# Two-block transformer on one core: norm sums of the last mixer taken at the end of the first expert stage, and the spatial unit's dense product placed behind the keys

## The chip, the cores and the metric

The kernel runs on one core of a Trainium2 chip. The metric is the device time of one execution in microseconds (us); less is better. The core has five engines that run side by side, each in the order of its own instruction list: TensorE (PE, with its weight loads shown apart as PEld), VectorE (DVE), ScalarE (ACT), GpSimd (POOL) and SyncE (SP). SP does no arithmetic here: it issues the weight transfers. An engine waits at an instruction until the semaphores that it needs have come, and everything behind it in its list waits too.

## The reference

Two blocks follow each other on the same 256 tokens of 1024 channels. Block A (two layers and a final rmsnorm with a gain) isn't touched. Block B has two layers; each runs a mixer and then a mixture of experts (16 experts, each takes 32 tokens). Layer 0 does it for the tokens `x` and for 256 context tokens `xc`; layer 1 takes from the context only keys and values.

```python
def rms_norm(x):
    return x * lax.rsqrt(jnp.mean(x * x, axis=-1, keepdims=True) + EPS)

def modulate_2(x, shift, scale):
    return rms_norm(x) * (1 + scale) + shift

x = rmsnorm(x_of_block_A, final_norm)          # end of block A
for l in range(2):
    hx = modulate_2(x, sh1, sc1);  hc = modulate_2(xc, csh1, csc1)
    px = hx @ w_in[l]              # columns u 256, v 256, f 256, q 256, kv 128, kr 64
    pc = hc @ w_in[l][:, col0:]    # last layer: kv and kr alone
    ya = gelu(u) * spatial(rms_norm(gelu(v)))  # spatial unit
    yb = fft2(f).real
    q  = rope(rms_norm(rms_norm(px_q) @ w_uq))
    k, v = rms_norm(px_kv) @ w_ukv, ...        # tokens and context
    x  = x + g1 * (concat(ya, yb, attention(q, k, v)) @ w_out[l])
    x  = x + g2 * expert_choice_moe(modulate_2(x, sh2, sc2), ...)
    # layer 0 does the last lines for xc too
```

At the start of block B's layer 0 two norms follow each other: the final rmsnorm of block A, with a gain, and the rms_norm of the mixer.

## The kernel before

Activations are held transposed: `xT` and `xcT` are 128 partitions (channels within a group) by 8 groups of channels by 256 tokens, in fp32. A dense product is done with split operands: `split` (L314, L315) makes from 1024 columns of a weight a rounded part `wsh` on ACT and the rest `wsl` on DVE, and `mm3` makes three matmuls of each pair of tiles (L322 high by high, then L323 and L324 with one low part each). There are two buffers each for `wsh` and `wsl`, so a third split waits until PE has used up the first.

Block B is driven by a plan, one string for each layer (`PLAN`, L53 and L54), whose words are traced in their order. `x0` and `x1` make the modulated norms of tokens and context; `v0` the dense product with the weight `wvf` (columns v and f); `u0` that with `wu` (the spatial unit's u); `tj` the one with `wqk` (the low-rank columns q, kv, kr) for tokens and context; `nj` the norms of these low-rank rows and their transposes (L1337 to L1360); `fj` the Fourier product; `k1` and `k0` keys and values of context and tokens (L1371 to L1401); `q0` the queries (L1418 to L1440); `a..` one head of attention (from L1504); `sj`, `w0`, `p0`, `r0` the spatial product, the output product, the router's norm and the routing. `F` fills in products of modulation vectors (L473, evicted at L477 or L479). A scheduler then sets the order in which each engine runs the traced instructions, so a word that is moved in one layer's plan, and a sum that is traced elsewhere, can move instructions of the other stages too.

A norm's sums of squares are made by `sums` (L608 on): eight Squares on ACT (L615), eight fp32 matmuls with a block of ones (L617), which the trace records as two each, a transpose on DVE (L619), one matmul that gathers (L621). `inv_sqrt` (L627) and `rsqrt` (L594 to L606, nine small DVE operations) follow, then `spread` (a COPY, L637, and a transpose, L639, on DVE). `modulated` multiplies on DVE (L664), adds the shift on ACT (L665, `hh`) and takes the low part on DVE (L666, `hl`).

In layer 0 the two norms are done as one chain on the tokens: sums of x, first inverse root `y1`, sums of x times the gain, second inverse root from `y1` and these. The first inverse root also rescales `xT` in place (L1592).

Expert weights come in pieces of 2 MB through a ring of buffers (`slot`, L281); SP issues a transfer (L294) when the buffer's last reader is done. At the end of layer 0's expert stage each half of the last results is added to `xT` and then `xcT` (L1891).

## Time and profile before

| | us |
|---|---|
| median of 3 runs | 1552.39 (1551.93 to 1553.54) |
| profiled execution | 1550.65 |
| its span, first to last instruction | 1548.9 |
| PE busy | 1425.8 (92%) |
| DVE busy | 894.8 (58%) |
| ACT busy | 578.5 (37%) |
| 16 DMA engines moved | 434.09 MB, mean 280 GB/s |
| mean granted TensorE clock | 0.975 of full |

In the span, block A runs to about 700 us. Block B's layer 0 begins its mixer there and its experts at about 940; layer 1 begins at about 1190, its experts at 1347. Times in the rows are us from the span's start. In a row of a timeline the first number is the start, the second the time until the last of its instructions ended, then engine, line, operation, output and inputs (buffer numbers left out), shapes and how many instructions the row holds; in brackets, how long the engine had been idle before and what it waited for. One matmul's time includes its passage through the array, so the distance of two starts is what it costs in a row of matmuls.

### The profile page before, as it was taken

The page shows a single profiled execution, that of the slowest core. Times are in us where ns is not written, and L with a number is a line of the kernel's source. Part 1 is how long each engine was busy: PE and PEld are TensorE (multiplying, and loading weights), DVE is VectorE, ACT ScalarE, POOL GpSimd, SP SyncE. Part 2 cuts the span into 40 slices and gives each one's busy share as a digit, 9 for nine tenths or more (in the row PEclk, how much of TensorE's full clock was granted, in tenths as well). Part 3 has the DMA queues.
Part 4 walks back from the last instruction along what each step waited for, and adds up shares of the span by engine and source line. Part 5 has one row for each costly group of instructions (what it writes and reads, how often), then busy time and mean ns, then how long its engine had stood idle before and what let it go on. Part 6 is the DMA issues. An engine that isn't in the chain of part 4 may idle for free.

```text
span 1548.9 us, 25284 instructions
## 1 busy us (share of the span) xinstructions
PE 1425.8 (92%) x10360; PEld 990.0 (64%) x10362; DVE 894.8 (58%) x2051; ACT 578.5 (37%) x1180; POOL 5.0 (0%) x15
## 2 busy tenths in 40 slices
PE   5999999999999999999999999999998889897665
PEld 2965899997967999996754784443433656632111
DVE  5668788896776998966665542322224765422011
ACT  3455444443555444544654441211102564310000
POOL 0000000000000000000000000000000000000000
PEclk9999999999999999999999999999999999999788
DMA  9647678597424866554286976899993225699998
GB/s 396 261 178 297 261 275 323 216 394 302 179 110 162 313 259 233 210 210 171 113 315 252 404 305 251 329 414 388 415 368 162 110 109 198 276 428 428 427 427 341
DMA packets 33666, 434.09 MB, mean 280 GB/s; under 512 B 3728, under 2 KB 4368, under 8 KB 6032
## 3 DMA queue, kind: packets, MB, share of 16 engines
q1 hardware_dynamic: 32400, 429.92, 69.8%
q10 hardware_dynamic: 1152, 2.57, 0.5%
q8 instruction: 81, 1.33, 0.3%
q14 instruction: 33, 0.27, 0.0%
HBM read 431.43 MB, written 1.05 MB: 279 GB/s over the span
## 4 chain that ended last, share of the span: by engine, by line
PE 75%; DMA 10%; DVE 9%; ACT 2%; issue 1%; POOLq 0%; DVEq 0%; ACTq 0%; SPq 0%
PE g L322 13%; PE g L324 13%; PE g L323 13%; PE g L1838 7%; PE y L1875 5%; DMA raw<-in_md_dram 4%; PE t L473 3%; DMA raw<-in_mgu_dram 3%; DMA h<-in_mgu_dram 3%; DVE wsl L315 2%; PE m L1838 2%; PE t L1797 2%; PE y L1506 1%; PE g L1523 1%; PE y L1504 1%
## 5 line engine op out<-in xcount | busy, mean ns | idle before, releaser
L314 ACT ACTIVATE wsh<-raw 128x1024 fp32r<-128x1024 f32 (+4 forms) x236 | 242.8, 1033 | 316.4 <-PE g L323 233.9
L315 DVE TENSOR_TENSOR wsl<-raw,wsh 128x1024 fp32r<-128x1024 f32 (+4 forms) x236 | 279.5, 1188 | 88.9 <-ACT wsh L314 88.2
L322 PE MATMUL g<-h,wsh 128*128 128x256 f32 x1072 | 303.8, 286 | 3.7 <-ACT h L657 2.4
L324 PE MATMUL g<-h,wsl 128*128 128x256 f32 x1072 | 304.1, 285 | 2.0 <-DVE wsl L315 2.0
L323 PE MATMUL g<-h,wsh 128*128 128x256 f32 x1072 | 303.9, 285 | 0.2
L322 PEld LDWEIGHTS g<-h,wsh 128*128 128x128 f32 x1072 | 205.1, 192 | 9.5 <-ACT h L665 3.2
L324 PEld LDWEIGHTS g<-h,wsl 128*128 128x128 f32 x1072 | 205.6, 192 | 3.9 <-DVE wsl L315 2.8
L323 PEld LDWEIGHTS g<-h,wsh 128*128 128x128 f32 x1072 | 205.9, 192 | 1.4 <-DVE h L666 0.6
L1838 PE MATMUL g<-raw,xs 128*32 128x512 f32 x1232 | 165.2, 626 | 20.4 <-DMA raw<-in_mgu_dram 19.8
L1875 PE MATMUL y<-raw,a 128*32 128x512 f32 x736 | 99.9, 631 | 9.3 <-DMA raw<-in_md_dram 8.4
L1838 PEld LDWEIGHTS g<-raw,xs 128*32 128x32 f32 x1232 | 38.8, 112 | 106.6 <-issue 70.4
L324 PE MATMUL g<-gh,wsl 128*128 128x256 f32 x352 | 99.8, 284 | 1.5 <-DVE wsl L315 1.5
L322 PE MATMUL g<-gh,wsh 128*128 128x256 f32 x352 | 100.1, 284 | 0.0
L323 PE MATMUL g<-gl,wsh 128*128 128x256 f32 x352 | 99.8, 283 | 0.0
L438 DVE CUSTOM_DVE_ANT_0 raw<-raw,crowc,cols 128x1024 f32<-128x1024 f32 x64 | 80.7, 1280 | 1.2 <-DMA raw<-in_mod1t_dram 1.1
L473 PE MATMUL t<-raw,zc 128*32 128x512 f32 x512 | 71.4, 611 | 6.9 <-DMA raw<-in_mod_dram 6.9
L1802 ACT ACTIVATE xs<-t,modada,ra 128x128 f32<-128x128 f32 x32 | 14.6, 457 | 151.3 <-PE t L1797 107.7
L324 PEld LDWEIGHTS g<-gh,wsl 128*128 128x128 f32 x352 | 67.5, 192 | 1.9 <-DVE wsl L315 1.9
L322 PEld LDWEIGHTS g<-gh,wsh 128*128 128x128 f32 x352 | 67.5, 192 | 1.6 <-issue 1.2
L323 PEld LDWEIGHTS g<-gl,wsh 128*128 128x128 f32 x352 | 67.5, 192 | 0.8 <-issue 0.8
L1875 PEld LDWEIGHTS y<-raw,a 128*32 128x32 f32 x736 | 23.7, 113 | 64.3 <-issue 42.6
L1800 DVE TENSOR_SCALAR xs<-t,ra,modada 128x128 f32<-128x128 f32 x32 | 13.1, 410 | 87.6 <-PE t L1797 50.4
(480 smaller groups left out, 2327.3 us busy)
## 6 DMA issues: line engine op xcount, KB each, us to landing
raw<-in_mgu_dram SPq DMA_DIRECT2D x61, 2048.0 KB, 13.7
raw<-in_md_dram SPq DMA_DIRECT2D x28, 2048.0 KB, 12.0
raw<-in_ffgu_dram SPq DMA_DIRECT2D x22, 2048.0 KB, 8.9
raw<-in_ada_dram SPq DMA_DIRECT2D x19, 2048.0 KB, 7.8
raw<-in_mod_dram SPq DMA_DIRECT2D x12, 2048.0 KB, 9.5
raw<-in_mod1t_dram SPq DMA_DIRECT2D x11, 2048.0 KB, 9.7
raw<-in_ffd_dram SPq DMA_DIRECT2D x16, 1408.0 KB, 7.1
raw<-in_win_dram SPq DMA_DIRECT2D x6, 2048.0 KB, 12.6
```

Of the source, the lines that this page charges most:

```text
L314: self.nc.scalar.activation(hi, src, AF.Copy)
L315: self.nc.vector.tensor_tensor(lo, src, hi.bitcast(F32), op=ALU.subtract)
L322: mm(out, ah, bh, start=first, stop=False)
L323: mm(out, ah, bl, start=False, stop=False)
L324: mm(out, al, bh, start=False, stop=last)
L438: nc.vector.tensor_tensor_reduce(junk, w[:, q, :], zr[:, i, :], 0.5, self.cols[:, o + 4 * s + q:o + 4 * s + q + 1], ALU.mult, ALU.add, m[: ...
L473: nc.tensor.matmul(acc[32 * j:32 * j + 32, :], zw[:, k, :], w[:, k, :], start=(k < 4), stop=(k >= 4))
L1504: nc.tensor.matmul(sc, self.qT[:, hd, ts], self.kT[:, hd, :nk], start=True, stop=False)
L1506: nc.tensor.matmul(sc, self.qrT[s2, hd // 2, ts], self.krT[s2, hd // 2, :nk], start=False, stop=True)
L1797: nc.tensor.matmul(ps, s["ht"][:, t, k * 128:(k + 1) * 128], oh[:, t, :], start=(t == 0), stop=(t == 1))
L1838: nc.tensor.matmul(banks[si][u][32 * e:32 * e + 32, :], xs[:, k, e * 32:e * 32 + 32], raw[:, u * 2048 + e * 512:u * 2048 + e * 512 + 512], ...
L1875: nc.tensor.matmul(ys[si][32 * e:32 * e + 32, :], hts[si][:, f * 128 + 32 * e:f * 128 + 32 * e + 32], raw[:, (fj * 4 + e) * 512:(fj * 4 + ...
```

## The change

Three things are done, all in block B.

1. Sums for layer 1's mixer are traced at the end of layer 0's expert stage, behind the last addition to `xT` and behind that to `xcT` (`sums2`). They use another form: each squared tile is the stationary operand, 128 by 128, and a two-column selector the moving one, so the sums of 256 tokens come out as 128 by 2, with the mean and epsilon already in; `spread2` takes the inverse root on these two columns (one DVE operation fewer) and spreads it by two matmuls with a broadcast operand into PSUM, from where `modulated` reads it. The DVE transposes and the COPY of `sums` and `spread` go in these two places. A word `E` at the plan's start makes the first two splits of `wvf`.
2. In layer 0 the two roots no longer depend on each other. With a prepared gain `gfin`, the root of g squared plus epsilon, the combined norm needs one sum alone; the first norm's sum, which rescales `xT`, is traced behind it.
3. `u0` stands behind `k0` in layer 1's plan, in front of `q0`, where it stood in front of `tj`. The transfer of `wu` moves with it: SP issues it behind `wqk` and `sm` (the weights of the attention's projections) instead of in front of them, and half of `wo` lands in the buffer `h` instead of a ring buffer.

```diff
-EX = 0
...
 PLAN = ['F1 +Q x1 x0 tj +U F2 nj uj v0 ...
-        '+U x0 x1 v0 u0 +H +Q F2 tj nj F1 +A1 -A fj k1 k0 F1 q0 a03 F1 sj F5 a02 a00 F1 a01 -B3 p0 w0 -W2 r0']
+        'E +U x0 x1 v0 +H +Q F2 tj nj F1 +A1 -A fj k1 k0 u0 F1 q0 a03 F1 sj F5 a02 a00 F1 a01 -B3 p0 w0 -W2 r0']
...
+        self.epsc = self.t(c, [128, 2], F32, "epsc")
+        nc.vector.memset(self.epsc, EPS)
+        self.sel2 = self.t(c, [128, 2, 2], F32, "sel2")
+        nc.vector.memset(self.sel2, 0.0)
+        for t in range(2):
+            nc.vector.memset(self.sel2[:, t, t:t + 1], 1.0)
...
+        nc.vector.tensor_tensor(self.gfin, g, g, op=ALU.mult)
+        nc.vector.tensor_scalar(self.gfin, self.gfin, EPS, None, op0=ALU.add)
...
+        self.rsqrt(y, c, t, c)
+        nc.vector.tensor_tensor(self.gfin, self.gfin, y, op=ALU.mult)
...
+    def sums2(self, x):
+
+        nc = self.nc
+        ps = self.ps(self.stag)[:, :2]
+        nk = x.shape[1]
+        nc.tensor.matmul(ps, self.ident, self.epsc, start=True, stop=False)
+        for k in range(nk):
+            sq = self.w([128, 256], "a256", NA2)
+            nc.scalar.activation(sq, x[:, k, :], AF.Square, scale=1.0 / 32)
+            for t in range(2):
+                nc.tensor.matmul(ps, sq[:, t * 128:t * 128 + 128], self.sel2[:, t, :], start=False, stop=(k == nk - 1 and t == 1))
+        return ps
+
+    def spread2(self, cp):
+
+        y = self.w([128, 2], "rsy2", 2)
+        self.rsqrt(y, cp, self.w([128, 2], "rst2", 2), self.w([128, 2], "rsc2", 2))
+        r = self.ps("y")[:, :256]
+        for t in range(2):
+            self.nc.tensor.matmul(r[:, t * 128:t * 128 + 128], y[:, t:t + 1].to_broadcast([128, 128]), self.ident, start=True, stop=True)
+        return r
...
-            w = self.split(raw[:, k0 * 512:(k0 + 2) * 512], 1024)
+            w = self.pre.pop(0) if self.pre else self.split(raw[:, k0 * 512:(k0 + 2) * 512], 1024)
...
-            self.h[1] = self.hc if l == 0 else self.modulated(xc, self.scale_cols(mn, 1, None, 1), mn, 0, 1, later=VX > 0)
+            r = self.spread2(self.early.pop(1)) if l else None
+            self.h[1] = self.hc if l == 0 else self.modulated(xc, self.scale_cols(mn, 1, None, 1), mn, 0, 1, r=r, later=VX > 0)
...
-            r = (self.rx if EX == 2 else self.spread(self.inv_sqrt(self.rx, 1024))) if EX else None
+            r = self.spread2(self.early.pop(0))
...
-            y1 = self.inv_sqrt(self.sums(x), 1024)
-            s2 = self.sums(x, gain)
-            v = self.w([128, 8], "rsc2", 1)
-            nc.vector.tensor_tensor(v, y1, y1, op=ALU.mult)
-            nc.vector.tensor_tensor(v, v, s2, op=ALU.mult)
-            y2 = self.inv_sqrt(v, 1024)
-            nc.vector.tensor_tensor(y2, y2, y1, op=ALU.mult)
-            r2 = self.spread(y2)
+            r2 = self.spread(self.inv_sqrt(self.sums(x, self.gfin), 1024, EPS * EPS))
+            s1 = self.sums(x)
...
-            r1 = self.spread(y1)
+            r1 = self.spread(self.inv_sqrt(s1, 1024))
...
+            elif c == "E":
+                self.mark("b TM1")
+                self.pre = [self.split(self.raw("wvf")[:, i * 1024:i * 1024 + 1024], 1024) for i in range(2)]
...
-                    if EX and q == 3 and n == 1 and si == 0:
+                    if q == 3 and n == 1:
 
                         self.stag = ST[1]
-                        self.rx = self.rstd(x, 1024) if EX == 2 else self.sums(x)
+                        self.early[si] = self.sums2(x)
```

How the engines' lists change in the places that matter, before and after. Names: `y_11848` (before) holds the tokens' sums in PSUM, `y_11873` (after) the context's, `rsy` and `rsc` the small operands of the root, `wsl_..` low weight parts, `xcT_65` the context.

DVE between the last addition to the context and the first norm products of layer 1, before:

```order
L1891 SCALAR_TENSOR_TENSOR xcT_65<-t_11816,modada_630_4212,xcT_65 128x256
L619 STREAM_TRANSPOSE a_1975_11873<-y_11848 128x256
L315 TENSOR_TENSOR wsl_11980<-raw_2008_11975,wsh_11979 128x1024
L627 TENSOR_SCALAR rsc_11877<-t_11875 128x8
L315 TENSOR_TENSOR wsl_12000<-raw_2008_11975,wsh_11999 128x1024
L596 TENSOR_SCALAR rsy_11879<-rsc_11877 128x8
L597 TENSOR_SCALAR rsy_11879<-rsy_11879 128x8
...
L606 SCALAR_TENSOR_TENSOR rsy_11879<-rsc_11877,rsy_11879 128x8
L637 COPY a_1980_11890<-rsy_11879 128x256
L639 STREAM_TRANSPOSE rsr_11892<-a_1980_11890 128x256
L664 SCALAR_TENSOR_TENSOR a_1982_11894<-xT_61,acol_11844,rsr_11892 128x256
```

The same place after (L1930 is L1891 of before, L613 to L623 are L596 to L606, L703 is L664):

```order
L1930 SCALAR_TENSOR_TENSOR xcT_65<-t_11869,modada_636_4235,xcT_65 128x256
...
L621 SCALAR_TENSOR_TENSOR rsc_1993_11943<-rst_1992_11942 128x2
L621 SCALAR_TENSOR_TENSOR rsc_1993_11943<-rsc_1993_11943,rst_1992_11942 128x2 x2
L613 TENSOR_SCALAR rsy_2006_11992<-y_11873 128x2
L623 SCALAR_TENSOR_TENSOR rsy_1991_11941<-rsc_1993_11943,rsy_1991_11941 128x2
L614 TENSOR_SCALAR rsy_2006_11992<-rsy_2006_11992 128x2
L616 TENSOR_TENSOR rst_2007_11993<-rsy_2006_11992 128x2
L617 TENSOR_TENSOR rst_2007_11993<-rst_2007_11993,y_11873 128x2
L314 TENSOR_TENSOR wsl_11931<-raw_1983_11928,wsh_11930 128x1024
L314 TENSOR_TENSOR wsl_11935<-raw_1983_11928,wsh_11934 128x1024
L703 SCALAR_TENSOR_TENSOR a_1998_11960<-xT_61,acol_11956,y_11953 128x256
```

The first operation of the context's root, `rsy_2006` from its sums `y_11873`, now stands in front of the last operation of the tokens' root, and two weight splits stand between that root and the first norm product.

PE around the keys and queries of layer 1, before (L1379 values, L1396 and L1400 transposes of the first keys, L1418 queries):

```order
L1400 MATMUL t_12479<-cons_66,a_2117_12471 128x128 x2
L1396 MATMUL t_12486<-cons_66,kk_12448 128x128 x4
L1400 MATMUL t_12492<-cons_66,a_2120_12484 128x128 x2
L1379 MATMUL y_12516<-raw_2066_12314,cq_12389 128x512
L1418 MATMUL y_12572<-raw_2066_12314,cq_12378 128x384 x2
L1418 MATMUL y_12580<-raw_2066_12314,cq_12378 128x384 x2
L1418 MATMUL y_12589<-raw_2066_12314,cq_12389 128x384 x2
```

After (L1435 and L1439 are those transposes, L1418 the values, L1457 the queries, L1474 their transposes; `y_12529` and `y_12564` are the two halves of u):

```order
L1435 MATMUL t_12439<-cons_66,kk_12401 128x128 x4
L1439 MATMUL t_12445<-cons_66,a_2110_12437 128x128 x2
L1418 MATMUL y_12469<-raw_2056_12267,cq_12342 128x512
L321 MATMUL y_12529<-hh_1996_11958,wsh_12525 128x256
L322 MATMUL y_12529<-hl_1997_11959,wsh_12525 128x256
...
L322 MATMUL y_12564<-hl_1997_11959,wsh_12560 128x256
L323 MATMUL y_12564<-hh_1996_11958,wsl_12561 128x256
L1457 MATMUL y_12597<-raw_2056_12267,cq_12331 128x384 x2
L1474 MATMUL t_12636<-cons_66,qq_12596 128x128 x2
L1457 MATMUL y_12605<-raw_2056_12267,cq_12331 128x384 x2
```

The 48 matmuls of u (two halves of 24) stand between the last values and the first query, with the transposes of the second tile's keys among them; before, they stood in front of the low-rank products.

PE at the end of layer 0's low-rank products, before (`y_8294` is the first quarter of u):

```order
L323 MATMUL m_8049<-wsl_8135,hh_1240_7998 128x448
L324 MATMUL m_8049<-wsh_8134,hl_1241_7999 128x448
L473 MATMUL t_8179<-raw_1270_8177,zc_1198_7872 32x512 x3
L322 MATMUL y_8294<-h_7145,wsh_8290 128x256
L323 MATMUL y_8294<-h_7145,wsh_8290 128x256
L324 MATMUL y_8294<-h_7145,wsl_8291 128x256
```

After (L490 is L473, L1397 is L1358):

```order
L323 MATMUL m_8068<-wsh_8153,hl_1243_8005 128x448
L490 MATMUL t_8186<-raw_1273_8184,zc_1204_7895 32x512 x3
L490 MATMUL t_8198<-raw_1275_8196,zc_1204_7895 32x512 x8
...
L1397 MATMUL t_8240<-cons_66,a_1287_8237 128x128
L1397 MATMUL t_8251<-cons_66,a_1290_8248 128x128 x2
L1397 MATMUL t_8288<-cons_66,a_1301_8285 128x128
L1397 MATMUL t_8299<-cons_66,a_1304_8296 128x128
L321 MATMUL y_8313<-h_7168,wsh_8309 128x256
L322 MATMUL y_8313<-h_7168,wsh_8309 128x256
```

Eleven modulation products instead of three, and the eight transposes of the low-rank rows, now stand in front of u; before, the transposes stood among u's matmuls.

ACT at the same place, before (L1337 to L1341 sums of the low-rank rows, L314 a split; `raw_1302` holds `wu`):

```order
L1337 ACTIVATE a_1274_8191,ss_8190<-g_8046 128x256
L1340 ACTIVATE a_1274_8191,ss_8190<-g_8046 128x128
L1341 ACTIVATE a_1274_8191,ss_8190<-g_8046 128x64
L314 ACTIVATE wsh_8290<-raw_1302_8288 128x1024
L1337 ACTIVATE a_1277_8199,ss_8190<-g_8047 128x256
L1337 ACTIVATE a_1289_8241,ss_8240<-g_8048 128x256
```

After (L1376 to L1380 those sums, L1390 and L1391 the scaled rows, L1399 the transposes' copies; `raw_1307` holds `wu`):

```order
L1380 ACTIVATE a_1296_8266,ss_8259<-m_8068 128x64
L1390 ACTIVATE a_1287_8237<-g_8065,ry_1285_8226 128x256
...
L1390 ACTIVATE a_1304_8296<-m_8068,ry_1299_8274 128x256
L1391 ACTIVATE a_1304_8296<-m_8068,ry_1299_8274 128x128
L313 ACTIVATE wsh_8309<-raw_1307_8307 128x1024
L313 ACTIVATE wsh_8375<-raw_1307_8307 128x1024
L765 ACTIVATE a_1311_8338<-y_8313 128x256
```

The split of u's weight stood in front of most of the sums; now both splits stand behind all sums, scaled rows and copies.

## Rows read from the trace of the kernel before

**Rows 1.** Stretches: us, busy us of PE, PEld, DVE, ACT, POOL, then clock, DMA, GB/s.

```profile
733.00:748.00 15.00, 14.93 (x116) 13.53 (x111) 8.62 (x32) 9.18 (x29) 0.00 (x0) 1.00 0.71 281
940.00:1190.00 250.00, 245.18 (x1941) 98.21 (x1940) 68.81 (x148) 35.05 (x66) 0.39 (x1) 1.00 0.88 357
1196.00:1202.00 6.00, 0.39 (x2) 0.30 (x2) 5.62 (x18) 0.23 (x1) 0.00 (x0) 0.80 0.00 0
1202.00:1206.00 4.00, 3.67 (x9) 2.86 (x10) 4.00 (x11) 2.69 (x7) 0.00 (x0) 0.50 0.03 6
1264.00:1276.00 12.00, 9.52 (x41) 5.63 (x42) 10.29 (x37) 8.03 (x19) 0.00 (x0) 1.00 0.00 0
1370.00:1530.00 160.00, 113.25 (x718) 33.99 (x717) 24.43 (x44) 8.73 (x17) 0.00 (x0) 0.87 1.01 427
```

**Rows 2.** Timeline of PE from the end of layer 0's experts into layer 1's mixer.

```profile
1196.45 0.39 PE L621 MATMUL t<-a,cons 128*128 128x8 f32 x2 [1.09 <-DVE a L619]
1202.34 0.80 PE L322 MATMUL g<-wsh,hh 128*128 128x512 f32 x1 [5.49 <-ACT hh L665]
...
1207.17 0.62 PE L617 MATMUL y<-a,ones 128*32 128x256 f32 x2
...
1220.90 0.39 PE L324 MATMUL g<-wsh,hl 128*128 128x512 f32 x1
1221.12 0.28 PE L322 MATMUL y<-hh,wsh 128*128 128x256 f32 x1
1221.24 0.28 PE L323 MATMUL y<-hl,wsh 128*128 128x256 f32 x1
...
1229.57 0.25 PE L322 MATMUL g<-wsh,h 128*128 128x192 f32 x1
```

**Rows 3.** All weight loads of L621: duration min/median/max in ns.

```profile
L621 PEld LDWEIGHTS t<-a,cons x18: 186/189/272, 11.6 to 1215.1; 128*128 128x128 f32 x18
```

**Rows 4.** Timeline of DVE in the same stretch and in the low-rank products.

```profile
1195.17 0.88 DVE L1891 SCALAR_TENSOR_TENSOR xcT<-t,modada,xcT 128x256 f32<-128x256 f32 x2 [0.50 <-PE t L1889]
...
1196.33 1.18 DVE L315 TENSOR_TENSOR wsl<-raw,wsh 128x1024 fp32r<-128x1024 f32 x1
...
1201.25 1.28 DVE L664 SCALAR_TENSOR_TENSOR a<-xT,acol,rsr 128x256 f32<-128x256 f32 x3
...
1238.31 1.09 DVE L315 TENSOR_TENSOR wsl<-raw,wsh 128x896 fp32r<-128x896 f32 x1
```

**Rows 5.** Timeline of PE, third quarter and end of layer 1's low-rank products.

```profile
1239.45 0.35 PE L323 MATMUL g<-wsl,h 128*128 128x192 f32 x1 [0.61 <-DVE wsl L315]
...
1246.78 0.37 PE L324 MATMUL m<-wsh,hl 128*128 128x448 f32 x1
```

**Rows 6.** Timeline of PE, keys, queries and the first attention score of layer 1.

```profile
1264.79 1.13 PE L1379 MATMUL y<-raw,cq 128*128 128x512 f32 x2 [1.32 <-ACT a L1375]
1265.77 2.85 PE L1418 MATMUL y<-raw,cq 128*128 128x384 f32 x8
...
1275.91 1.02 PE L1504 MATMUL y<-kT,qT 128*128 128x512 f32 x2
```

**Rows 7.** Timeline of PE, layer 0: modulation products, low-rank products, u, v.

```profile
713.09 2.76 PE L473 MATMUL t<-raw,zc 128*32 128x512 f32 x18
716.33 0.47 PE L322 MATMUL g<-wsh,hh 128*128 128x448 f32 x1 [0.48 <-ACT hh L665]
...
732.59 1.06 PE L473 MATMUL t<-raw,zc 128*32 128x512 f32 x6
...
747.66 0.40 PE L322 MATMUL g<-wsh,hh 128*128 128x512 f32 x1
```

**Rows 8.** Timeline of ACT, layer 0: split of u, gelu, last scaled low-rank row.

```profile
733.07 1.09 ACT L314 ACTIVATE wsh<-raw 128x1024 fp32r<-128x1024 f32 x1
...
736.76 0.39 ACT L726 ACTIVATE a<-y 128x256 f32<-128x256 f32 x1 [1.99 <-PE y L324]
...
741.13 0.37 ACT L1352 ACTIVATE a<-m,ry 128x128 f32<-128x128 f32 x1
```

## What the change does to the time

> **What bounds the kernel now.** I read the table of stretches first. From 1370 to 1530 us the DMA engines are busy all the time (share 1.01, 427 GB/s) while PE works 113 of 160 us [rows 1]: the end is set by the expert weights of layer 1, and these can only start to flow fast when that stage's first buffers come free, so a shift of layer 1's mixer moves the whole queue, and with it the end, by the same amount. Before, it is PE: 245 of 250 us in layer 0's experts, 14.93 of 15 in layer 0's products of u [rows 1]. What PE gains or loses in layer 0's mixer is therefore carried on. Between the two stages lies the one long hole that the change goes for: from 1196 to 1202 PE works 0.39 us, DVE 5.62 [rows 1].
>
> The PE timeline shows the hole's shape: after the gathering matmul at 1196.45 nothing until the first v product at 1202.34, 5.49 us idle [rows 2]. DVE fills it with the root chain: last addition to the context ending at 1196.05, two weight splits of 1.18, nine root operations, COPY and transpose, first norm product at 1201.25 [rows 4]. Then PE runs at half its clock (granted 0.50, that is 1.2 GHz) until about 1206 [rows 1]. v ends at 1221.12, u takes from there to 1229.57, the low-rank products end at 1247.15 [rows 2, 5].
>
> **Layer 1, the hole.** The new form takes the tokens' sums out of the hole, since they are done on PE among the last expert results. COPY and transpose go. But the context's sums come in: eight squared tiles, two fp32 matmuls each, all in front of the tokens' spread on PE, and the tokens' last root operation stands on DVE behind the first one of the context. The trace of before has no matmul of this shape. The nearest is the gathering one, L621: a 128 by 128 fp32 stationary tile, 8 moving columns, 0.28 to 0.39 us as a pair of records [rows 2]; its two weight loads of 189 ns [rows 3] fill it. At 0.28, sixteen are 4.5 us. They start when the last context result is out (about 1195.3), so they end at 1199.8; last root operation 0.2, spread 0.6, and meanwhile DVE makes two splits (2.4 us from about 1200.8): first norm product 1203.3, first v product 1204.4, 2.1 later than now. The lower bound is that they hide behind ACT's eight Squares (done about 1197.4): then DVE reaches the norm products at 1201.3 as now, cost 0. I take 2.1.
>
> In this shape each squared tile is loaded as weights to serve two columns. The Trainium skill, page "TensorE: Matmul & The Clock Gate", section "LDWEIGHTS (loading the stationary operand)", says that a load costs by its columns alone, the column count over 1.2 in ns, 107 for 128. Two loads per matmul would be an estimate of 0.21 us and 3.4 us for the sixteen, and the first v product 1.1 earlier. The trace doesn't bear it out for fp32: the same load takes 189 ns at the median [rows 3].
>
> The word `E` I price at nothing: the two splits are made in the hole already [rows 4].
>
> **Layer 1, v.** Now 18.8 us (1202.34 to 1221.12) [rows 2]. In it stand the context's eight sum matmuls, 0.62 each and about 0.1 for the change of operand, 6 us in all [rows 2]; they go. What remains is 48 matmuls at 0.22 [rows 2], 10.6, and some 2 for the half clock: 12.8. DVE must in that time make sixteen norm operations of 0.43 (1.28 for three) [rows 4] and two more splits: 1203.3 + 6.9 + 2.4 = 1212.6, and two quarters of PE work follow its last but one split, so it ends at 1217 by either way. That is 4.1 earlier.
>
> **Layer 1, low-rank products.** They follow v at once, the 8.45 us of u are gone, so by PE alone (17.6 us now [rows 2, 5], less stalls of 2) they would end at 1232.4. But DVE is late: the third quarter waits for its split, made at 1238.31 to 1239.40, now 18.3 us behind v's end [rows 4, 5]. Out of these 18.3 go u's two splits (2.4) and u's gelu (six operations of about 0.37, 2.2): 13.7 remain, the third split would be done at 1230.7, and the end comes 7.7 later as now (1239.45 to 1247.15) [rows 5]: 1238.4. Adding up the DVE operations one by one from 1212.6, with context norms begun earlier, gives 1236.8. I take 1237.2, 10 earlier than now; the ends are 1232.4 (14.8 earlier) and 1241 (6 earlier, if nothing of the context's norm is done sooner).
>
> **Layer 1, u in its new place.** 48 matmuls at 0.12 [rows 2] are 5.8 us in front of the queries. In the 11.1 us from the last values (1264.79) to the first score (1275.91) [rows 6] PE is busy 9.5 of 12 and DVE 10.3 of 12 [rows 1]: the queries share DVE with the keys of the second tile. With u in front, that key work is done beside u, and the queries run alone afterwards, which gives back some 2 us. I take a cost of 4; the ends are 3.3 (all of PE's 2.5 idle is used) and 8.45, what u took in its old place with its waits for splits. Layer 1 together: -10 + 4 = -6, between -11.5 and +2.5.
>
> Wu's later transfer costs nothing: the DMA engines are idle from 1264 to 1276 [rows 1], and its splits stand on ACT and DVE ahead of the keys.
>
> **Layer 0.** The second root chain no longer waits for the first. PE had filled that wait with nine modulation products (eighteen records, 713.09 to 715.85) and context products, so only 0.48 us was idle [rows 7]. Eight of the nine now stand behind the low-rank products, so these start, and end, up to 2.9 earlier (2.45 for the eight and 0.48); I take 2.7, an end at 729.9 instead of 732.6.
>
> Behind it the order has got worse. Eleven modulation products take 3.6 us (three take 1.0 [rows 7]). Now u starts at 733.6, its first split being made among the sums, and PE is full to 747.66 [rows 1, 7], where four matmuls of v, 0.9 us, are already done, so u ends at 746.7 in effect. After the change both splits of u stand on ACT behind the last scaled row. That row ends now 8.9 us behind the low-rank products (741.50) [rows 7, 8]; without the split (1.09) and one gelu (0.84) ahead of it, 7.0. Then the split's two parts, 1.09 and 1.18, and u's other 92 matmuls of 0.12: 729.9 + 7.0 + 2.3 + 11.0 = 750.2, against 746.7: 3.5 late. Nothing behind it on PE is idle to take this up. The ends: 2.9 early (the splits come in time after all) and 6.2 late (the products don't end earlier).
>
> **Start of the program.** Some fifteen small DVE operations for the constants stand where PE and DVE wait for the first weights: nothing.
>
> **Sum.** -6 + 3.5 = -2.5, on the profiled execution's 1550.65 a time of 1548.1. That execution lies 1.7 below the median of its three runs; against the median the forecast is 1552.4 - 2.5 = 1549.9, and with the lighter ends of the unknown costs (the sums of the context may hide, the queries may gain more) lying nearer than the heavier, I say 1549.5.
>
> **Rivals.**
> *Layer 0 costs nothing.* The chain of sums, rows and copies on ACT finishes sooner than I think, since no gelu stalls it (1.99 us of waiting is in the row at 736.76 [rows 8]), and u follows the modulation products closely. Then -6 - 2.9 = -8.9, 1543.5. Against it: u's first matmul can't start before ACT has worked through four scaled rows and six copies.
> *They cancel.* u in its new place costs its old 8.45: -10 + 8.45 + 3.5 = +2, 1554.4; with the low-rank end at its lower bound and u at 4, +1.5.
> *Slower: u in front of the queries is a new stall.* Its place is the chain last values, queries, scores. It adds there two splits (2.3 on ACT and on DVE), two gelus (2.2 on DVE) and 5.8 on PE; DVE is at 86% there already [rows 1]. If these come one after another, the price is about 12, and the sum -10 + 12 + 3.5 = +5.5, 1557.9. It decides from a price of 9.6 on. For it: the wait lines of the keys name ACT [rows 6]. Against it: the first split stands far ahead, and gelu isn't needed by the queries.
> *The change doesn't do what it says* in one place: the sums are begun in the expert stage, but the context's half runs in the hole. This is in the sum.
>
> **How the numbers follow.** Forecast 46%, its own range 1546 to 1553; layer 0 free 18%; cancelled 12%; slower 24%. What a measurement of this kernel can tell from no change is 0.2%, 3.1 us. The forecast lies at its edge and I share it 24 to 22 between faster and same; with the others: faster 42%, same 34%, slower 24%. The range, 1542.5 to 1557.5, leaves out the far part of the first and the last rival.
>
> **What would show it.** In the new trace: the first v product of layer 1 at about 1204 less the shift by layer 0, with the sixteen matmuls of the context's sums in front of it at 0.28 each (0.13 would show my price wrong); no sum matmul among v; v 12.8 us long; the low-rank products' third quarter waiting for DVE; u between values and queries at 0.12 a matmul, and the first score 4 us later behind the low-rank end than now. In layer 0: PE idle some 4 us in front of u, its first matmul waiting for ACT's split. The forecast is wrong if that idle time is missing (then faster), or if PE waits within or behind u in layer 1 for more than 3 us (then slower).

## The result: slower, by 10.6 us

The changed kernel takes 1562.98 us (median of 5 runs, 1562.20 to 1563.29) against 1552.39 (5 runs, 1550.68 to 1553.71): a ratio of 1.0066, 95% interval 1.0053 to 1.0079. The forecast was 1549.5 and faster; the time lies above the range, and 5 us above the one rival on the slower side. The profiled execution took 1563.19 (span 1561.4, mean granted clock 0.970 against 0.975), 12.5 more than the one of before.

Where these 12.5 arise, read from the PE and DVE timelines of the two executions, always from start to start. "Start" is the first of the last four additions to the tokens in layer 0's experts (1190.83 before, 1197.38 after).

| us | before | after | difference | predicted |
|---|---|---|---|---|
| block A's last addition | 699.0 | 699.6 | +0.6 | 0 |
| from there to the first output product added in layer 0 (to the context) | 175.8 | 181.4 | +5.6 | +3.5 |
| from there to "start" | 316.0 | 316.4 | +0.4 | 0 |
| start to first v product of layer 1 | 11.5 | 18.0 | +6.5 | +2.1 |
| start to last v matmul | 30.1 | 33.0 | +2.9 | -4.1 |
| start to last low-rank matmul | 55.9 | 52.5 | -3.4 | -10 |
| start to first attention score | 85.1 | 90.4 | +5.4 | -6 |
| start to first output product added in layer 1 | 119.0 | 124.3 | +5.3 | -6 |
| from there to the last addition to the tokens | 235.4 | 236.1 | +0.7 | 0 |

Rows four to eight are running sums from "start", so the whole is made of rows one, two, three, eight and nine: 0.6 + 5.6 + 0.4 + 5.3 + 0.7 = 12.6. Both layers lose; a shift of the mixer of layer 1 reaches the end undiminished, as [rows 1] had suggested.

**The profile after.** The table of stretches, to hold against [rows 1] (columns as there):

```profile
732.00:747.00 15.00, 11.98 (x75) 8.64 (x68) 6.88 (x21) 7.81 (x22) 0.00 (x0) 0.89 0.85 309
1200.00:1204.00 4.00, 4.00 (x21) 4.00 (x21) 1.60 (x4) 2.56 (x7) 0.00 (x0) 0.52 0.02 4
1204.00:1208.00 4.00, 4.00 (x21) 4.00 (x20) 2.17 (x10) 2.69 (x6) 0.00 (x0) 0.50 0.00 0
1212.00:1216.00 4.00, 1.39 (x6) 1.00 (x6) 3.99 (x7) 1.20 (x3) 0.00 (x0) 0.50 0.01 2
1370.00:1530.00 160.00, 115.11 (x768) 37.04 (x764) 26.00 (x49) 9.07 (x18) 0.00 (x0) 0.91 1.01 428
```

The hole of before, 0.39 us of PE work in 6, is filled: PE works 4.00 of 4. But it works at a clock of 0.50, half of what it was granted a few us earlier, and a new hole stands at 1212 to 1216. PE's timeline there, which answers to [rows 2]:

```profile
1197.13 1.93 PE L635 MATMUL y<-sel,a 128*128 128x2 f32 x16
...
1201.40 0.85 PE L635 MATMUL y<-sel,a 128*128 128x2 f32 x4
...
1205.24 5.97 PE L635 MATMUL y<-sel,a 128*128 128x2 f32 x28
1211.52 1.22 PE L644 MATMUL y<-cons,rsy 128*128 128x128 f32 x4 [0.32 <-DVE rsy L623]
1215.36 0.79 PE L321 MATMUL g<-wsh,hh 128*128 128x512 f32 x1 [2.62 <-ACT hh L704]
...
1220.64 0.42 PE L321 MATMUL g<-wsh,hh 128*128 128x512 f32 x1
```

L635 is the new two-column matmul. The first sixteen records (eight matmuls) go at 0.24 us a matmul, at full clock. Then the spacing is 0.43: the last fourteen matmuls take 5.97 us behind the last expert result. The first v products, to 1220.64, run at half clock too, at 0.43 apart in place of 0.23. DVE meanwhile, which answers to [rows 4]:

```profile
1201.64 0.48 DVE L1930 SCALAR_TENSOR_TENSOR xcT<-t,modada,xcT 128x256 f32<-128x256 f32 x1 [0.80 <-PE t L1928]
1202.92 0.48 DVE L1930 SCALAR_TENSOR_TENSOR xcT<-t,modada,xcT 128x256 f32<-128x256 f32 x1 [0.80 <-PE t L1928]
...
1211.24 0.16 DVE L613 TENSOR_SCALAR rsy<-y 128x2 int32<-128x2 int32 x1 [3.83 <-PE y L635]
1211.32 0.15 DVE L623 SCALAR_TENSOR_TENSOR rsy<-rsc,rsy 128x2 f32<-128x2 f32 x1
...
1212.01 2.36 DVE L314 TENSOR_TENSOR wsl<-raw,wsh 128x1024 fp32r<-128x1024 f32 x2
1214.29 1.26 DVE L703 SCALAR_TENSOR_TENSOR a<-xT,acol,y 128x256 f32<-128x256 f32 x3
```

The last additions come 1.28 us apart, each waiting for an expert result behind two sums; then DVE stands 3.83 us in front of the context's first root operation (L613), and the tokens' last one (L623), which needs nothing more, is queued behind it. Two splits follow, and only then the first norm product.

The low-rank products end at 1249.90 + 0.37; a low part again waits for its split, as in [rows 5] (0.95 us, at 1242.57), and twice PE waits for DVE's gelu of v (L769):

```profile
1233.50 0.36 PE L321 MATMUL g<-wsh,h 128*128 128x192 f32 x1 [1.08 <-DVE vv L769]
1236.17 0.44 PE L321 MATMUL g<-wsh,hh 128*128 128x448 f32 x1 [1.31 <-DVE vv L769]
1242.57 0.36 PE L322 MATMUL g<-wsl,h 128*128 128x192 f32 x1 [0.95 <-DVE wsl L314]
1249.90 0.37 PE L323 MATMUL m<-wsh,hl 128*128 128x448 f32 x1
```

From the last values to the first score, which answers to [rows 6], it is now 20.05 us (1267.76 to 1287.81) against 11.12. PE, then DVE:

```profile
1267.76 1.45 PE L1418 MATMUL y<-raw,cq 128*128 128x512 f32 x2 [1.32 <-ACT a L1414]
1268.74 0.68 PE L321 MATMUL y<-hh,wsh 128*128 128x256 f32 x1
1269.22 0.42 PE L322 MATMUL y<-hl,wsh 128*128 128x256 f32 x1
...
1277.37 0.28 PE L323 MATMUL y<-hh,wsl 128*128 128x256 f32 x1
1278.39 1.56 PE L1457 MATMUL y<-raw,cq 128*128 128x384 f32 x4 [0.74 <-DVE ug L769]
...
1287.81 1.02 PE L1543 MATMUL y<-kT,qT 128*128 128x512 f32 x2
```

```profile
1277.91 0.42 DVE L769 SCALAR_TENSOR_TENSOR ug<-a,y 128x256 f32<-128x256 f32 x1 [0.48 <-ACT a L768]
...
1279.74 1.23 DVE L314 TENSOR_TENSOR wsl<-raw,wsh 128x1024 fp32r<-128x1024 f32 x1
1280.88 0.41 DVE L769 SCALAR_TENSOR_TENSOR ug<-a,y 128x256 f32<-128x256 f32 x1
1281.21 0.55 DVE L1461 TENSOR_REDUCE sk<-a 128x2 f32<-128x384 f32 x1
```

u itself takes 8.7 us, its first fourteen matmuls 0.21 apart and not 0.12. The first query waits for u's gelu (L769), and another split and the second gelu stand on DVE in front of the queries' norm (L1461).

In layer 0, PE and ACT, which answer to [rows 7, 8]:

```profile
731.35 2.77 PE L490 MATMUL t<-raw,zc 128*32 128x512 f32 x22
...
737.86 0.33 PE L1397 MATMUL t<-cons,a 128*128 128x128 f32 x1 [0.72 <-ACT a L1391]
739.43 0.58 PE L321 MATMUL y<-h,wsh 128*128 128x256 f32 x1 [0.62 <-ACT wsh L313]
...
753.90 0.28 PE L323 MATMUL y<-hh,wsl 128*128 128x256 f32 x1
```

```profile
738.06 0.38 ACT L1391 ACTIVATE a<-m,ry 128x128 f32<-128x128 f32 x1
738.31 2.02 ACT L313 ACTIVATE wsh<-raw 128x1024 fp32r<-128x1024 f32 x2
```

The picture is the one forecast: u waits for a split that stands behind ACT's last scaled row.

### The profile page after: what moved, and what is told of

The parts are those of the page before. It is cut to its first block, busy times and chain, and to the rows that moved or that the text cites. A ratio compares the mean times of both kernels' runs of the same rounds, so it can differ in the third digit from the quotient of the medians.

```text
span 1561.4 us, 25375 instructions
## 1 busy us (share of the span) xinstructions
PE 1438.3 (92%) x10402; PEld 1004.9 (64%) x10402; DVE 894.7 (57%) x2057; ACT 581.0 (37%) x1180; POOL 5.0 (0%) x15
## 4 chain that ended last, share of the span: by engine, by line
PE 78%; DVE 8%; DMA 8%; ACT 3%; issue 1%; ACTq 0%; DVEq 0%; SPq 0%
PE g L321 13%; PE g L323 13%; PE g L322 13%; PE g L1877 8%; PE y L1914 5%; PE t L490 3%; DMA raw<-in_mgu_dram 3%; DMA raw<-in_md_dram 3%; DMA h<-in_mgu_dram 3%; PE t L1836 2%; PE m L1877 2%; DVE wsl L314 2%; PE y L1545 1%; PE g L1562 1%; PE y L1543 1%
## 5 line engine op out<-in xcount | busy, mean ns | idle before, releaser
L313 ACT ACTIVATE wsh<-raw 128x1024 fp32r<-128x1024 f32 (+4 forms) x232 | 238.4, 1032 | 310.2 <-PE g L322 226.9
L314 DVE TENSOR_TENSOR wsl<-raw,wsh 128x1024 fp32r<-128x1024 f32 (+4 forms) x232 | 274.9, 1190 | 88.2 <-ACT wsh L313 87.1
L1877 PE MATMUL g<-raw,xs 128*32 128x512 f32 x1216 | 162.7, 623 | 19.6 <-DMA raw<-in_mgu_dram 19.1
L490 PE MATMUL t<-raw,zc 128*32 128x512 f32 x512 | 73.3, 627 | 5.3 <-DMA raw<-in_mod_dram 5.3
L1886 ACT ACTIVATE a<-g 128x512 f32<-128x512 f32 x12 | 7.2, 597 | 148.4 <-PE g L1877 148.4
## 6 DMA issues: line engine op xcount, KB each, us to landing
raw<-in_md_dram SPq DMA_DIRECT2D x30, 2048.0 KB, 12.5
```

What stands on the lines that cost most here:

```text
L313: self.nc.scalar.activation(hi, src, AF.Copy)
L314: self.nc.vector.tensor_tensor(lo, src, hi.bitcast(F32), op=ALU.subtract)
L490: nc.tensor.matmul(acc[32 * j:32 * j + 32, :], zw[:, k, :], w[:, k, :], start=(k < 4), stop=(k >= 4))
L1877: nc.tensor.matmul(banks[si][u][32 * e:32 * e + 32, :], xs[:, k, e * 32:e * 32 + 32], raw[:, u * 2048 + e * 512:u * 2048 + e * 512 + 512], ...
```

## The experiments

In each, all that isn't named is as in the kernel before (the constants of the new code apart). Ratios are to the kernel before, on the same chip. Stage times come from one profiled execution; the control, the first below, shows how far such a one can be off.

**consts_only.** All three parts undone, only the preparation of `epsc`, `sel2` and `gfin` left.

> All three parts undone; what stays of the change is the preparation at the program's start (about fifteen small operations for epsc, sel2 and gfin). Theory (the prediction's term 'start of the program'): nothing, a ratio of 1.000 within 0.1%, the last addition of block A between 696 and 701 us in the profile as in all the others, first score of layer 1 at 85.1 behind the last token updates as before. Rival: the preparation shifts block A by 1 to 3 us, which would then stand in every kernel here and in the sum of the whole change; ratio 1.001 to 1.002, last addition of block A 1 to 3 us later.

1553.38 us (11 runs) against 1552.44, 1.0002 [0.9993, 1.0011]. The preparation costs nothing that can be measured. Its profile has the first score 86.9 behind "start" and not 85.1. In it TensorE's granted clock is 0.50 in a part of u (1225.0 to 1228.4) and u takes 9.7 us; the profile of before has no such stretch in u, which takes 8.3. So two executions of the same order differ by 1.8 us there, and a difference below 2 us between the stage times of two profiles shows nothing by itself.

**only_sums2.** Part 1 alone, without `E`.

```diff
-        'E +U x0 x1 v0 +H +Q F2 tj nj F1 +A1 -A fj k1 k0 u0 F1 q0 ...
+        '+U x0 x1 v0 u0 +H +Q F2 tj nj F1 +A1 -A fj k1 k0 F1 q0 ...
+            y1 = self.inv_sqrt(self.sums(x), 1024)     # layer 0 as before
```

> The kernel before with part 1 alone (sums2 and spread2 for tokens and context; u in its old place; no E). Theory (the context's sixteen two-column matmuls and the tokens' sixteen run at the half clock, about 0.43 us each, in front of the first v product, and the half clock then lasts into v): the first v product about 6.5 us later behind the last expert matmul, v's end about 3 later, the time about 3 us slower, 1555. Rival (the loss is in u's new place, and the sums as such gain what the forecast said): first v product 2 later, v's end 4 earlier, 4 us faster, 1548.

1557.31 us (6 runs), 1.0040 [1.0028, 1.0052]. First v product 16.9 behind start (before 11.5), v's end 35.8 (30.1), u 13.6 us long (8.3), first score 94.0 (85.1); 5 us slower where I had expected 3. The part that was to bring the gain loses by itself, through two things: the sums and u. On PE (the sums, then u's second half) and in the table of stretches:

```profile
1196.00 5.97 PE L635 MATMUL y<-sel,a 128*128 128x2 f32 x28
...
1226.93 0.28 PE L323 MATMUL y<-hh,wsl 128*128 128x256 f32 x1
1228.18 0.47 PE L321 MATMUL g<-wsh,h 128*128 128x192 f32 x2 [0.97 <-DVE a L767]
...
1232.67 0.58 PE L321 MATMUL y<-hh,wsh 128*128 128x256 f32 x1 [1.77 <-DVE ug L769]
```

```profile
1192.00:1196.00 4.00, 4.00 (x21) 4.00 (x20) 1.45 (x3) 2.21 (x7) 0.00 (x0) 0.50 0.02 4
1196.00:1200.00 4.00, 4.00 (x21) 4.00 (x20) 1.69 (x9) 2.79 (x5) 0.00 (x0) 0.50 0.00 0
```

**sums2_wide.** only_sums2 with the selector broadcast to 128 moving columns; the same sums, each 64 times over.

```diff
-        ps = self.ps(self.stag)[:, :2]
+        ps = self.ps(self.stag)[:, :128]
-  nc.tensor.matmul(ps, self.ident, self.epsc, start=True, stop=False)
+  nc.tensor.matmul(ps, self.ident, self.epsc[:, 0:1].to_broadcast([128, 128]), start=True, stop=False)
...
-  nc.tensor.matmul(ps, sq[:, t*128:t*128+128], self.sel2[:, t, :], ...
+  nc.tensor.matmul(ps, sq[:, t*128:t*128+128], self.sel2[:, t, :].unsqueeze(2).to_broadcast([128, 2, 64]), ...
-        return ps
+        return ps[:, 0:128:64]
```

> As only_sums2, but each sum matmul moves 128 columns (each selector column repeated 64 times) instead of two; the same weight loads and the same sums. Theory (TensorE's clock falls because PE moves only two columns per load; with 128 it stays at 1.00 and a pair of records takes 0.25 to 0.30 us instead of 0.43): granted clock 1.00 in the 12 us behind the last expert products, first v product at least 2.5 us earlier than in only_sums2 (where it starts 16.9 us behind the first of the last token updates), the time some 3 us lower than only_sums2. Rival (the fp32 weight loads or the waiting are what lets the clock fall): half clock in the same stretch, time as only_sums2, 1557.

1545.15 us (4 runs), 0.9952 [0.9937, 0.9967], 12 us below only_sums2, where I had expected 3. First v product 11.4, v's end 25.5, first score 83.4. PE and the stretches:

```profile
1193.93 3.06 PE L635 MATMUL y<-sel,a 128*128 128x128 f32 x26
1197.80 0.68 PE L644 MATMUL y<-cons,rsy 128*128 128x128 f32 x4 [0.81 <-DVE rst L617]
```

```profile
1190.00:1194.00 4.00, 4.00 (x38) 4.00 (x37) 2.22 (x8) 3.80 (x8) 0.00 (x0) 1.00 0.02 4
1194.00:1198.00 4.00, 3.19 (x29) 3.02 (x29) 3.77 (x15) 1.55 (x5) 0.00 (x0) 1.00 0.01 2
```

A matmul of 128 columns takes 0.24 us (13 in 3.06), as one of two columns does at full clock; and the clock stays at 1.00 through the sums. (From 1198 to 1202, around the start of v, it is 0.79.) The other kernels below agree: with 128 columns the granted clock is 1.00 around the sums in change_wide (1201 to 1212.7) and in wide_ctxcopy (1188 to 1200); with two it is 0.50 in the changed kernel (1201 to 1220) and in sums2_copy (1192 to 1211). u is still slow here, 12.8 us from first to last matmul.

**early_ones.** Part 1's place with the old form (`sums`, `inv_sqrt`, `spread`).

```diff
-                        self.early[si] = self.sums2(x)
+                        self.early[si] = self.sums(x)
-            r = self.spread2(self.early.pop(1)) if l else None
+            r = self.spread(self.inv_sqrt(self.early.pop(1), 1024)) if l else None
...
-            r = self.spread2(self.early.pop(0))
+            r = self.spread(self.inv_sqrt(self.early.pop(0), 1024))
```

> As only_sums2, but the sums that are traced at the end of the expert stage keep the form of before: ones stationary, the squared tile moving, transposes and COPY on DVE (tokens and context). Theory (it is the form that costs: two moving columns per weight load let TensorE's clock fall to half, granted 0.50 from 1200 us on): the clock stays at 1.00 through the sums, the first v product comes at most 2 us later than before, v is 6 us shorter, the time 3 to 5 us faster than before. Rival (it is the place: any sums of the context in front of v's first product delay it): no better than only_sums2, 1555.

1548.17 us (8 runs), 0.9974 [0.9964, 0.9985]. The place is a gain; it was the form that lost. First v product 14.0, though v's end 27.1: the sums come out of v here too.

**sums2_copy.** only_sums2, `spread2`'s result copied by ACT from PSUM to SBUF.

```diff
-        return r
+        rs = self.w([128, 256], "rsr", NRS)
+        self.nc.scalar.activation(rs, r, AF.Copy)
+        return rs
```

> As only_sums2, but the spread root is copied by ACT from PSUM to SBUF, so its bank is free at once. Theory (there are two banks of that kind; the context's spread holds one until its last norm product, 14 us, and u's four products, which want both, take 13.6 us instead of 8.3): u takes 8 to 9 us again, the low-rank products end 4 to 5 us earlier than in only_sums2, the time 1553. Rival (u is slow there for the half clock and for its splits alone): u stays above 12 us, time as only_sums2, 1557.

1551.11 us (10 runs), 0.9989 [0.9978, 1.0001]. u takes 5.9 us and not 13.6; the first v product comes at 19.0, two later than in only_sums2. The copy is not the limit there: it is done at 1206.3 and DVE's first norm product starts at 1207.5, behind two weight splits where only_sums2 has one; the last addition comes 0.9 later, too. So u was held by its PSUM bank: `spread2` writes to the pool "y", which has two, and the context's spread occupies one until its last norm product on DVE. In only_sums2 that product starts at 1239.51:

```profile
1239.51 0.48 DVE L703 SCALAR_TENSOR_TENSOR a<-xcT,acol,y 128x256 f32<-128x256 f32 x1
```

Until then u's two halves share the other bank, so the second half waited for the gelu of the first (the 1.77 us above). It then ran at half clock, 0.21 us a matmul and not 0.12, which is some 2 us of the 13.6.

**only_u0.** Part 3 alone.

> The kernel before with part 3 alone (u behind the keys, its transfer behind wqk and sm). Theory (u's place in front of the queries costs 8.9 us, as much as u took in its old place, 8.45, since the queries wait for u's matmuls, partly at half clock, for its second split and for PSUM that its gelu frees): between same and 2 us slower, 1552 to 1555. Rival (it costs 4 there, the rest in the changed kernel came from elsewhere): 4 us faster, 1548.

1557.12 us (6 runs), 1.0032 [1.0019, 1.0044]: 5 us slower, worse than either of the two that I had expected. From the last values to the first score it is 20.08 us, the 8.9 of the changed kernel again. The low-rank products end only 4.3 earlier, though u's 8.3 us are gone in front of them, and the first score comes 4.4 later. PE waits in them for DVE, above all for the gelu of v:

```profile
1230.09 0.33 PE L321 MATMUL g<-wsh,h 128*128 128x192 f32 x1 [1.01 <-DVE vv L769]
1232.66 0.44 PE L321 MATMUL g<-wsh,hh 128*128 128x448 f32 x1 [1.46 <-DVE vv L769]
```

**u_behind_queries.** Part 3 alone, with `u0` one word further on.

```diff
-  ... fj k1 k0 u0 F1 q0 a03 F1 ...
+  ... fj k1 k0 F1 q0 u0 a03 F1 ...
```

> As only_u0, but u stands behind the queries (q0 u0 instead of u0 q0). Theory (in front of the queries u costs its full 8.7 us since keys, u and queries follow one another; behind them the first attention score comes 4 us earlier than in the kernel before, and u's 5.8 us of matmuls come into a stretch where PE is full): 1.5 to 3 us slower than before, 1554 to 1555. Rival (the cost is in the stages behind, by the later weights and their buffers): as only_u0, 1557.

1565.48 us (4 runs), 1.0084 [1.0069, 1.0099]: my theory missed by far. The scheduler put u in front of the first score, which then waited for u's gelu, and the scores that follow ran at half clock, 1.0 us a matmul; in only_u0 it is 0.53:

```profile
1282.48 2.08 PE L1543 MATMUL y<-kT,qT 128*128 128x512 f32 x2 [3.29 <-DVE ug L769]
1284.49 2.07 PE L1545 MATMUL y<-krT,qrT 64*128 64x512 f32 x2
```

```profile
1283.00:1293.00 10.00, 10.00 (x11) 2.50 (x10) 2.80 (x9) 2.15 (x5) 0.00 (x0) 0.50 0.00 0
```

**only_gfin.** Part 2 alone.

> The kernel before with part 2 of the change alone (one root chain in layer 0, the constants at the start). Theory (from the two traces: layer 0 grows by 5.6 us, block A by 0.6, because u's two weight splits stand behind all low-rank norms on ACT and PE then runs u's first matmuls at half clock): about 6 us slower, 1558. Rival (the 5.6 us belong to the other parts, whose tracing order moves layer 0 too): within 3 us of before. The forecast's own term was 3.5 slower.

1555.90 us (10 runs), 1.0021 [1.0012, 1.0030]. Layer 0's stage is 182.1 against 175.8, which is the 6 us that I had expected; the medians differ by 3.6 alone. Layer 1 is as before, and block A is 2.4 us shorter in this profile, which no part touches.

**gfin_presplit.** only_gfin, with both splits of u traced ahead of the low-rank norms (a word `W` in front of `nj`).

```diff
+            elif c == "W" and not arg:
+                raw = self.raw("wu")
+                self.preu = [self.split(raw[:, i * 1024:(i + 1) * 1024], 1024) for i in range(2)]
...
-            w = self.split(raw[:, c * 1024:(c + 1) * 1024], 1024)
+            w = self.preu.pop(0) if self.preu else self.split(raw[:, c * 1024:(c + 1) * 1024], 1024)
```

> As only_gfin, but the two splits of u's weight are traced ahead of the norms of the low-rank rows in layer 0. Theory (the loss of gfin is u waiting for its splits behind these norms, 8 us of hardly used PE and 3 us of half clock): u follows the low-rank products within 2 us, layer 0's mixer takes 174 to 177 us instead of 182, the time 5 to 7 us below only_gfin, 1549 to 1551. Rival (it is the eight modulation products that moved behind the low-rank products, or the new order of the splits costs elsewhere): mixer above 179 us, time above 1553.

1553.74 us (10 runs), 1.0007 [0.9997, 1.0016]. The stage falls to 177.7: 4.4 of the 6.3 us come back; by the ratios it is 2.2 of 3.3 us, not the 5 to 7 that I had expected. So the splits behind the norms were the cause of about two thirds of the loss; the rest is within what two profiles differ by. Part 2 brings no gain even so: counted from block A's last addition the low-rank products end 2.9 us earlier than before, but fifteen modulation products (3.63 us) stand behind them where three stood, and u starts only 0.3 earlier:

```profile
728.96 3.63 PE L490 MATMUL t<-raw,zc 128*32 128x512 f32 x30
732.53 0.39 PE L321 MATMUL y<-h,wsh 128*128 128x256 f32 x1
```

**change_wide.** The whole change with the 128-column sums.

> The whole change (all three parts), with 128 moving columns in the sum matmuls instead of two. Theory (most of the forecast's error is the half clock under the two-column matmuls): the first v product 5 to 6 us earlier than in the changed kernel, no stretch at 0.50 among the sums, the time 5 to 8 us under the changed kernel's 1563, 1555 to 1558; still slower than before, by layer 0's 5 us and u's new place. Rival (the clock falls in the change's own order all the same, or DVE takes over as the limit of v and the low-rank products): 1561 to 1563.

1555.19 us (10 runs), 1.0009 [1.0000, 1.0019]. Against 1.0066 for the change as it is: the difference of the ratios, 0.0057 or 8.9 us, is the two columns' share of the loss in this kernel. First v product 11.6, v's end 25.3, low-rank end 44.8 (11.1 earlier than in the kernel before), but the first score 82.8: from the last values to the first score it takes 20.10 us, so of the 11.1 only 2.3 are left behind u and the queries, and layer 0's 6.2 eat these.

**wide_ctxcopy.** sums2_wide, with a copy for the context's spread alone.

```diff
             r = self.spread2(self.early.pop(1)) if l else None
+            if r is not None:
+                rs = self.w([128, 256], "rsr", NRS)
+                nc.scalar.activation(rs, r, AF.Copy)
+                r = rs
```

> The kernel before with part 1 in the wide form (as sums2_wide), and the context's spread root copied by ACT to SBUF so that its PSUM bank is free for u; the tokens' spread is read from PSUM. Theory (u took 12.8 us in sums2_wide for want of the bank): u 8 to 9 us, low-rank products end 3 to 4 us earlier than in sums2_wide, 1541 to 1543. Rival (DVE's list is the limit of the low-rank products anyway): as sums2_wide, 1545.

1539.07 us (4 runs) against 1553.38, 0.9901 [0.9885, 0.9918]: faster than both kernels, 14.3 us below that of before and 23.9 below the changed one's median. u 5.6 us long, low-rank end 47.6, first score 76.7.

**wide_ctxcopy_u_n.** The same with `u0` behind `nj`.

```diff
-        '+U x0 x1 v0 u0 +H +Q F2 tj nj F1 ...
+        '+U x0 x1 v0 +H +Q F2 tj nj u0 F1 ...
```

> As wide_ctxcopy, but u stands behind the low-rank norms (nj u0) instead of in front of the low-rank products. Theory (keys and queries are a chain in which any work of PE adds itself, but the norms in front of them leave PE idle): low-rank products end 4 us earlier, u then costs 5 to 6, the first score within 1.5 us of wide_ctxcopy, same time. Rival (u's place matters only in front of the queries, and here its matmuls hide beside the norms): 3 to 4 us under wide_ctxcopy.

1543.52 us (4 runs), 0.9932 [0.9917, 0.9946], 4.5 us worse: low-rank end 43.7, but first score 80.2. With its bank free, u costs less in its old place than behind the norms: its 5.6 us there make the low-rank end only 4.0 later. That it covers DVE's norms and splits, for which PE waits in the low-rank products, is my reading; no run separates it.

What stays open: the medians of the kernels with the sums early lie 2.5 to 6 us further below that of before than their stage times in layer 1 would have it (sums2_wide: first score 1.6 earlier, median 7.3 lower). Part of that stands in block A, which no part touches and which ends between 696.2 and 700.7 in the fourteen profiles, and part in the scatter that the control shows. No run separates them. Nor was `E` run by itself: with it, in the changed kernel, two splits stand in front of the first norm product and the first v product comes 1.1 us later than in only_sums2, which has one split there; with 128 columns the two orders differ by 0.2 (11.6 and 11.4).

## Why the prediction was wrong

*The step that failed first: the price of the context's sums.* "At 0.28, sixteen are 4.5 us", and the first v product 2.1 later. The price was too high for full clock (0.24) and too low for the clock that these matmuls got (0.43). Two things were not in it. The clock fell to 0.50 while these matmuls ran, and they, the last expert results and the spread (1.22 us for 0.6) all ran at half of it. And I let the sums start behind the last expert result, when those of the tokens and of the first context tiles stand between the results and delay them: the last addition ended 8.6 and not 5.2 behind start (7.2 in sums2_wide, so 2.0 of these 3.4 us are the matmuls themselves and 1.4 the clock). From there to the first v product it is 9.4 us instead of 6.3. Together 6.5 where I had 2.1. The sign that I had named for a wrong price was 0.13; the error lay on the other side. sums2_wide confirms it: with the same matmuls at full clock the first v product stands at 11.4, and change_wide gets back 8.9 of the 10.6 us.

One premise was wrong from the start, though no term hangs on it: the tokens' sums were not in the hole. Before, too, their matmuls ran among the last expert results, the first four of them here:

```profile
1190.54 0.64 PE L617 MATMUL y<-a,ones 128*32 128x256 f32 x8
```

What the tokens' chain loses in the hole are the transposes, the gathering matmul and the COPY; what the change moves is the context's sums, out of v.

*v.* 15.2 us from its first matmul to the next product, forecast 12.8 (18.8 before). That the sums go out of it was right; the half clock of its first twelve matmuls cost 2.4 and not 2, a wait for a split 0.9, and the context's spread, not priced, 0.6.

*The low-rank products* took 19.6 us from v's end, forecast 20.2. So DVE's lag was sized rightly, and the end came late by what v was late: -3.4 instead of -10. change_wide, where the clock holds through the sums, bears out both terms: v ends 4.8 earlier than before (forecast 4.1), the low-rank products 11.1 (forecast 10). What is left wrong there is u's place and layer 0.

*The second step that failed: u's new place,* priced at 4, measured 8.9 (20.05 against 11.12 us from the last values to the first score), and the same in only_u0 (20.08) and change_wide (20.10). Of this, u takes 8.7, not 5.8: half clock for its first fourteen matmuls (1.3), transposes of keys among them. "Gelu isn't needed by the queries" was false: it reads u from a bank of the pool that the queries write to, so the first one waited for it. The 2 us that I gave back never came; another split and the second gelu stand on DVE in front of the queries' norm. That was the slower rival's mechanism; its price of 12 was too high, its deciding point of 9.6 nearly reached. My own sign for it, PE waiting within or behind u for more than 3 us, didn't come (2.7 us): of the 8.9 us, 7.9 are more busy time of PE (17.4 against 9.4) and 1.0 more waiting (2.7 against 1.7). So there was hardly any idle time into which u could go. By itself part 3 makes the kernel 5 us slower (only_u0), about half of what the whole change loses.

*Layer 0* was right in kind, but too small in size: 5.6 for 3.5. The products start 1.7 earlier (715.20, by block A's end) and end 1.8 earlier, not 2.7. I overlooked the place of the first norm's sum on DVE. The combined root is spread by 708.2, but next in DVE's list is the transpose of the other sum, which the products don't need; DVE stands 5.26 us in front of it, and the first norm product is queued behind:

```profile
713.41 0.45 DVE L658 STREAM_TRANSPOSE a<-y 128x256 f32<-128x256 f32 x1 [5.26 <-PE y L656]
713.78 1.24 DVE L703 SCALAR_TENSOR_TENSOR a<-xT,acol,rsr 128x256 f32<-128x256 f32 x3
```

The wait is the same in only_gfin, gfin_presplit and change_wide; what it would give to move that transpose no run shows. And u runs at half clock for its first thirteen matmuls (1.2). With the 0.9 that the products end later than forecast, this is the miss of 2.1. only_gfin and gfin_presplit show the late splits as the cause of most of the stage's loss.

*The start of the program* cost nothing, as priced, and the shift was carried to the end in full, as [rows 1] said.

*What I failed to see in the code:* `spread2` leaves its result in one of two PSUM banks that u needs. In the change u stands elsewhere and doesn't meet it; in only_sums2 u takes 5 us longer than before. That fits the single parts losing more than the whole (1.0021, 1.0040 and 1.0032 make 1.0093, the whole 1.0066), though no run separates it.

## What to carry to other kernels

Price a new small matmul at either level of the clock, and look at what PE does around it: where the granted clock falls, as it did here to 0.50, the neighbours pay too. Here 128 moving columns cost no more than two (0.24 us) and the clock held. Before an operand is left in PSUM to save a copy, count the banks of its pool and who needs the next one. Moving a product out of a stage pays only as far as PE bounds that stage (here 4.3 of u's 8.3 us came back, in only_u0); read there which engine PE waits for, and in the new place whether its consumers share an engine or a bank with what follows. Where a sum is moved or added, look in each engine's list at what now stands in front of the operations that should start earlier.

## What the hardware showed that I had not expected

The clock fell, and stayed low, with PE fully busy. In the changed kernel PE worked without a pause from 1197 to 1200 at a granted 1.00, and at 0.50 from 1200.2 on. In only_sums2 PE worked 4.00 of 4 us in two successive stretches at a granted 0.50 (1.2 GHz), with two-column matmuls between expert results; with 128 columns and nothing else changed it worked 4.00 of 4 at 1.00 (2.4 GHz). In u_behind_queries it was 10.00 of 10 at 0.50 with 512-column scores behind a wait of 3.29 us. The Trainium skill, page "TensorE: Matmul & The Clock Gate", section "What's actually happening", lets the clock fall behind an idle stretch and rise with activity. That fits the hole of before [rows 1, 2]; these stretches do not fit it, as the records' busy time counts it, and the measurement decides. The distances of the matmuls bear the granted clock out: 0.43 us at 0.50 against 0.24 at 1.00, and 1.0 against 0.53 for the scores. Why the clock fell is not shown, only with which of the two forms it did.

The fp32 weight load takes longer at that clock: for L635 it takes 188 ns at least and 333 at the median in the changed kernel, where most of them ran at 0.50, and 191 at the median in sums2_wide, where all ran at 1.00 (lines in this order):

```profile
L635 PEld LDWEIGHTS y<-sel,a x64: 188/333/337, 1197.1 to 1210.8; 128*128 128x128 f32 x64
```

```profile
L635 PEld LDWEIGHTS y<-sel,a x64: 187/191/192, 1187.9 to 1196.6; 128*128 128x128 f32 x64
```
